# Branch A's gate product moved into the SSD stage, branch B's merge gate into pairs of seven products beside those of u

## The chip, the cores and the metric

The kernel runs on one core of one Trainium2 chip. The metric is the device time of one execution in microseconds (us); the time before is the median of three runs. The engines are named as in the profile: PE is TensorE's matmul, PEld its weight load, DVE VectorE, ACT ScalarE, POOL GpSimd, SP SyncE, which issues most of the loads.

## The reference, cut to what matters

One layer of three parallel branches for 576 tokens (512 of a prompt, 64 of a sample), with D = 1024. All columns that the branches need come from one product of the normed tokens with `w_in`:

```python
hn = _rmsnorm(x, norm_g)
proj = hn @ w_in
u, v, gate_a, z, xbc, dt_raw, q, gate_x, merge = jnp.split(proj, _split_points(IN_SIZES), axis=-1)
u = jax.nn.gelu(u, approximate=False)
v = _layernorm(jax.nn.gelu(v, approximate=False), ln_v_g, ln_v_b)
h_a = u * _gmlp_spatial(v, w_spatial, b_spatial) * jax.nn.silu(gate_a)       # branch A
...
h_b = _gated_group_rmsnorm(y.reshape(bsz, L, D_INNER).astype(x.dtype), z, ssd_norm_g)   # branch B
h_x = _mem_attention(q, mem_k, mem_v) * jax.nn.silu(gate_x)                  # branch X
g_a, g_b, g_x = jnp.split(jax.nn.sigmoid(merge), N_BRANCH, axis=-1)
m = g_a * (h_a @ w_proj_a) + g_b * (h_b @ w_proj_b) + g_x * (h_x @ w_proj_x)
return x + m @ w_out, ...
```

Two of these products matter here, each of 1024 columns: `gate_a` (branch A's gate, at column O_GA of `w_in`) and the second third of `merge` (the merge gate of branch B, at O_M + D).

## The kernel before

**Products.** Tokens and weights are each split into a high part and the rest, and a product of two tiles is made as high x high, high x rest and rest x high. The split of a weight tile is a cast on ACT (L98) and a subtraction on DVE (L99). A plain product of a tile of 128 columns with the 576 tokens is two halves of 288 tokens with 24 matmuls each (8 blocks of the inner size, three products of parts): 96 for two tiles. `wino` makes a pair of tiles, 256 columns, out of seven products of 12 matmuls each, 84 in all; for it DVE makes four sums of weight blocks (S, L904 to L907), all of these are split, sums of token blocks stand ready in `tT` (made once by `token_sums`, which also overwrites a quarter of `hn_hi` and `hn_lo`), and DVE and ACT put the seven results together (L935 to L947). `wino_th` is a `wino` followed by a tanh.

**Stage B** comes first, branch B's SSD in eight groups. Its PE order is written out by hand: the stage is a list of jobs (`conv_job` four to a group, for the next group; `z_job` two; `proj_job`; `gate_job`), each of two halves of 24 matmuls (line L167 in the rows). A job's weights are loaded two jobs ahead and split one job ahead. Between halves stand the small steps of the group's chunks, `w[0]` to `w[11]` of `steps`; the numbers in `PLACES` say after which half of the group each is put (without an entry: 0, 1, 2, 4, 5, 7 and so on). Groups 0 and 1 have 12 halves, the others 16. In the last group, which has no next group, four `gate_job`s stand where the others have convolutions, and four more follow in a tail, with the steps left of group 7 among them. Then the last round of `proj_job` (r = 3) makes the end of branch B's projection and stores it to a scratch in DRAM, `m_scr`, by way of ACT's queue (L766). Before, these `gate_job`s make the merge gate of branch B: their tanh stays in SBUF in buffers that are free by then (`gate_th`), and one DVE instruction per half in the last `proj_job`s (L764) applies it.

**Stage A** follows (from L870). The order here is the program's text, which a scheduler refines. It runs `v_block` (two, with `v_sample`), the memory's keys and values (`kv_block`, two, L1120), `v_norm` (L1141), the eight `spatial` steps (L1161) into `SP`, then four `ga_pair`, each two plain products of branch A's gate with its tanh and a DVE instruction per half (`gate2`), and a DVE instruction that multiplies `SP` by the gate (L1199), and then four `u_pair`: a `wino` of u, a gelu, the product with `SP` (L1204) and a split into `ha`. `token_sums` runs beside the first `ga_pair`. Then `m_sb` is loaded from `m_scr`, and pairs of branch A's merge gate and of its projection alternate.

After it come branch X, the merge and the output product; neither of them is touched.

**Line numbers.** The rows below and the first of each two pieces of order have the lines of the kernel before. In the changed kernel the helpers (L98, L99) and stage B stand two lines further down, `wino` one line. A plain product in stage A has the line L154, one of `wino`'s matmuls L925.

Of the kernel before, what the change touches and what calls it, by code (L numbers as in the profile page):

```python
# [42 lines left out]
def tile_hybrid_step(  # L43
# [144 lines left out]
    with ExitStack() as stb:  # L188
# [530 lines left out]
        def gate_job(jj):  # L719
            k = {}  # L720

            def load():
                if jj % 2 == 0:
                    gate_th["w", jj // 2] = load_block(w_in2, 0, KD, [(O_M + D + jj * P, 256)])

            def prep():
                k["w"] = wsplit(gate_th["w", jj // 2], KD, (jj % 2) * P)

            def half(f):
                if f == 0:  # L730
                    if jj < 3:
                        if jj == 0:
                            gate_th["x"] = pb.tile([P, 3, TW], F32, tag="xs", name="thx", bufs=2)
                        gate_th[jj] = gate_th["x"][:, jj, 0:T]
# [4 lines left out]
                S.activation(gate_th[jj][:, sl], ps, AF.Tanh, scale=0.5)
            return Job(load, prep, half)  # L740

        def proj_job(r, p):
# [10 lines left out]
            def half(j):  # L753
                jj = 2 * p + j
                w = [t[:, :, j * P:(j + 1) * P] for t in k["w"]]
                for f in range(2):
# [6 lines left out]
                    if r == 3:  # L763
                        V.scalar_tensor_tensor(dst, gate_th[jj][:, sl], 1.0, dst, ALU.add, ALU.mult)  # L764
# [112 lines left out]
    def token_sums(tile_):  # L877

        F = []
        for i, (k0, h) in enumerate(((0, 0), (0, 1), (4, 1), (4, 0))):  # L880
            sl = slice(h * HT, (h + 1) * HT)
            F.append(tile_().rearrange("p r t -> p (r t)").rearrange("p (k t) -> p k t", k=4))
            V.tensor_tensor(F[i], hn_hi[:, k0:k0 + 4, sl], hn_lo[:, k0:k0 + 4, sl], ALU.add)
        V.tensor_tensor(F[0], F[1], F[0], ALU.subtract)
        V.tensor_tensor(F[1], F[2], F[1], ALU.subtract)
        V.tensor_tensor(F[2], F[2], F[0], ALU.subtract)
        V.tensor_tensor(F[3], F[3], F[2], ALU.subtract)
        for i in range(3):
            split(F[i + 1], tT[:, i, 0], tT[:, i, 1])
        return F[0]  # L890
# [84 lines left out]
    with ExitStack() as sta:  # L975
# [177 lines left out]
        def tile_gemm(raw, j, xh, xl):  # L1153
            t = w_slot().rearrange("p r (k c) -> p r k c", k=KD)
            split(raw[:, :, j * P:(j + 1) * P], t[:, 0], t[:, 1])
            return gemm((t[:, 0], t[:, 1]), KD, xh, xl)

# [353 lines left out]
```

## Time and profile before

| | us |
|---|---|
| median of 3 runs (lowest, highest) | 1127.05 (1125.96, 1128.54) |
| the profiled execution: its own time | 1126.1 |
| the profiled execution: span from the first to the last instruction | 1124.4 |
| PE busy in the span | 1094.3 (97%) |
| DVE busy | 780.7 (69%) |
| ACT busy | 618.0 (55%) |
| mean granted TensorE clock | 0.998 |

The profiled execution's own time is 1.7 us more than its span, and 0.95 us under the median. Durations below come from this one execution. An idle time stands in brackets before the instruction that ended it, with what released that instruction.

### The profile page before, as it was taken

Reading aid. Unit: us, or ns where it says so; the run is one execution under the profiler, and the core shown is the slowest. Engines: PE = TensorE matmul, PEld = TensorE weight load, DVE = VectorE, ACT = ScalarE, POOL = GpSimd, SP = SyncE. Lnnn points to the kernel's source line nnn. Section 1 sums busy time; section 2 is a strip of 40 time slices with the busy share of each in tenths; the row PEclk is TensorE's granted clock in tenths of the full one; section 3 lists DMA queues with packets and bytes.
Section 4 is the critical chain, followed back from the end, with each engine's and each line's share of the span. In section 5 each row is a group of like instructions: output and inputs, shape, how many; then the busy total and the mean of one; then the engine's idle time right before and its main releaser. Section 6 shows DMA issues by size and latency. Waiting matters only on the chain.

```text
span 1124.4 us, 20432 instructions
## 1 busy us (share of the span) xinstructions
PE 1094.3 (97%) x8200; PEld 1017.2 (90%) x8200; DVE 780.7 (69%) x1444; ACT 618.0 (55%) x1291; POOL 25.0 (2%) x109
## 2 busy tenths in 40 slices
PE   5999999999999999999999999999999999999997
PEld 3999898999999998999999777999999998889776
DVE  5779797768687886876536536877965567765743
ACT  6466787768767576774542335425643336565421
POOL 1010000000000000000000000000000000000000
PEclk9999999999999999999999999999999999999999
DMA  5343535353544534354324325441352453556311
GB/s 175 114 102 113 152 107 150 115 146 83 166 130 128 131 100 137 99 164 131 99 95 158 133 75 178 150 150 39 112 198 97 155 162 113 151 160 215 133 47 75
DMA packets 160334, 144.38 MB, mean 128 GB/s; under 512 B 10152, under 2 KB 141264, under 8 KB 160240
## 3 DMA queue, kind: packets, MB, share of 16 engines
q1 hardware_dynamic: 137136, 125.60, 36.8%
q10 hardware_dynamic: 23104, 17.49, 4.9%
q8 instruction: 64, 1.05, 0.4%
q14 instruction: 30, 0.25, 0.1%
HBM read 123.61 MB, written 19.46 MB: 127 GB/s over the span
## 4 chain that ended last, share of the span: by engine, by line
PE 89%; DVE 4%; ACT 3%; DMA 2%; issue 1%; SPq 0%; ACTq 0%; DVEq 0%
PE acc L167 36%; PE acc L925 16%; PE acc L154 12%; PE acc L1055 4%; PE acc L1460 4%; PE acc L1120 2%; DMA e<-a_scr 2%; PE yps L555 1%; PE sps L651 1%; PE sps L510 1%; PE sps L574 1%; PE sps L599 1%; PE yps L1408 1%; PE yps L1161 1%; PE yps L1066 1%; PE sps L539 1%
## 5 line engine op out<-in xcount | busy, mean ns | idle before, releaser
L167 PE MATMUL acc<-hn_hi,whi 128*128 128x288 f32 x896 | 270.2, 302 | 0.2 <-DVE zs L471 0.2
L167 PE MATMUL acc<-hn_lo,whi 128*128 128x288 f32 x896 | 264.2, 295 | 0.0
L167 PE MATMUL acc<-hn_hi,wlo 128*128 128x288 f32 x896 | 264.0, 295 | 0.0
L167 PEld LDWEIGHTS acc<-hn_hi,whi 128*128 128x128 f32 x896 | 168.2, 188 | 2.3 <-issue 1.2
L167 PEld LDWEIGHTS acc<-hn_lo,whi 128*128 128x128 f32 x896 | 168.4, 188 | 0.4
L167 PEld LDWEIGHTS acc<-hn_hi,wlo 128*128 128x128 f32 x896 | 168.1, 188 | 0.1
L98 ACT CAST w<-wraw 128x1024 fp32r<-128x1024 f32 (+1 forms) x64 | 59.2, 942 | 103.3 <-PE acc L925 24.0
L99 DVE TENSOR_TENSOR wlo<-wraw,whi 128x1024 fp32r<-128x1024 f32 x72 | 87.9, 1221 | 30.3 <-ACT whi L98 29.8
L167 PE MATMUL acc<-hb,whi 128*128 128x288 f32 x512 | 104.6, 299 | 0.1
L98 ACT CAST whi<-wraw 128x1024 fp32r<-128x1024 f32 x72 | 75.6, 1050 | 41.3 <-PE acc L167 38.8
L99 DVE TENSOR_TENSOR w<-wraw,w 128x1024 fp32r<-128x1024 f32 x64 | 68.5, 1087 | 36.0 <-ACT w L98 35.8
L925 PE MATMUL acc<-hn_hi,w 128*128 128x288 f32 x512 | 89.5, 300 | 0.0
L925 PE MATMUL acc<-tT,w 128*128 128x288 f32 x576 | 86.1, 298 | 0.0
L426 DVE SCALAR_TENSOR_TENSOR cacc<-raw,cwh,cacc 128x600 f32<-128x600 f32 x96 | 80.5, 838 | 3.7 <-ACT cacc L424 2.8
L167 PEld LDWEIGHTS acc<-hb,whi 128*128 128x128 f32 x512 | 81.6, 188 | 1.0 <-issue 0.6
L925 PEld LDWEIGHTS acc<-tT,w 128*128 128x128 f32 x576 | 78.5, 188 | 0.9 <-issue 0.9
L925 PEld LDWEIGHTS acc<-hn_hi,w 128*128 128x128 f32 x512 | 74.0, 188 | 2.1 <-DVE thx L943 0.3
L167 PE MATMUL acc<-hb,wlo 128*128 128x288 f32 x256 | 75.3, 294 | 0.0
L99 DVE TENSOR_TENSOR w<-S,w 128x1024 fp32r<-128x1024 f32 x32 | 39.2, 1224 | 25.1 <-ACT w L98 25.1
L499 ACT ACTIVATE e<-e,nacs 128x128 f32<-128x128 f32 (+1 forms) x160 | 50.0, 382 | 8.6 <-DVE e L497 8.5
L154 PE MATMUL acc<-ha,w 128*128 128x288 f32 x384 | 51.6, 295 | 0.0
L154 PEld LDWEIGHTS acc<-ha,w 128*128 128x128 f32 x384 | 51.2, 189 | 0.0
(394 smaller groups left out, 2116.0 us busy)
## 6 DMA issues: line engine op xcount, KB each, us to landing
wraw<-in_w_in_dram SPq DMA_DIRECT2D x44, 1024.0 KB
wraw<-in_w_in_dram SPq DMA_DIRECT2D x16, 512.0 KB
e<-a_scr SPq DMA_DIRECT2D x32, 256.0 KB
h<-in_state_ssm_dram SPq DMA_DIRECT2D x16, 512.0 KB
out_dram<-h ACTq DMA_DIRECT2D x16, 512.0 KB
wraw<-in_w_proj_b_dram SPq DMA_DIRECT2D x8, 1024.0 KB
ebc<-e_scr SPq DMA_DIRECT2D x16, 288.0 KB
wraw<-in_w_mem_kv_dram SPq DMA_DIRECT2D x4, 1024.0 KB
```

The costliest lines, as they stand in the source:

```text
L98: S.copy(hi, v)
L99: (e or V).tensor_tensor(lo, v, hi, ALU.subtract)
L154: PE.matmul(ps[:n, :width], lhsT=a, rhs=b[:, sl], start=(i == 0), stop=(i == last))
L167: PE.matmul(ps[:, 0:HT], lhsT=a[:, k], rhs=b(k)[:, sl], start=(n == 0), stop=(n == 3 * nk - 1))
L426: V.scalar_tensor_tensor(a[:, 0:n], raw[:, i:i + n], cwh[:, i, q:q + 1], a[:, 0:n], ALU.mult, ALU.add)
L499: S.activation(e[:, h, 0:w], e[:, h, 0:w], AF.Exp, bias=nacs[:, c, h0_ + h:h0_ + h + 1])
L510: PE.transpose(tp[:, j * P:(j + 1) * P], xs[:, j, c0:c0 + P], ident)
L539: PE.matmul(cb[:, 0:w], lhsT=xs[:, 2, c0:c0 + P], rhs=CF[:, c0:c0 + w], start=True, stop=True)
L925: PE.matmul(ps[:, 0:HT], lhsT=w[:, r, k], rhs=x(q, k), start=first and n == 0, stop=n == 11, skip_group_check=True)
L1055: PE.matmul(pss[i], lhsT=x(k)[:, c], rhs=w[:, r, k2], start=(k + q == 0), stop=(k == KD - 1 and q == 2))
L1120: PE.matmul(pss[i], lhsT=x[xr], rhs=w[:, r, k2], start=(k + q == 0), stop=(k == KD - 1 and q == 2))
L1460: PE.matmul(ps[:, 0:cn], lhsT=x(k)[:, c], rhs=w, start=(k + q == 0), stop=(k == KD - 1 and q == 2))
```

## The change

**Branch A's gate** goes into stage B. `gate_job` now makes tiles of O_GA, plain; per half ACT makes the tanh, a DVE instruction the gate's value (the tanh plus one, times the product), and ACT's queue stores it to a new scratch `g_scr`, 16 stores in all. Tile 0 stands as the last job of group 0, tile 1 as the second of group 1, tiles 2 and 3 in group 7, and 4 to 7 in the tail. So groups 0 and 1 have 14 halves and group 7 has 12. In group 1 the last convolution job now closes the group, with z's second tile ahead of it. `PLACES` is new for group 1, group 2 takes the usual numbers, and in group 7 a step stands behind every half; `norm_y(7)` comes one half earlier in the tail.

**Branch B's merge gate** goes into stage A. `gate_b(p)` is a `wino_th` of O_M + D, a load of two tiles of `m_scr`, one DVE instruction that multiplies them, and a store to a new scratch `mb_scr`, from which `m_sb` is then loaded. It stands behind `u_pair(p)`, so that u and gate alternate. `u_pair` loads its part of `g_scr` and multiplies `SP` by it itself. The four `ga_pair` and the 16 DVE instructions of L764 are gone.

**Order in stage A.** `token_sums` runs behind the first v block, its splits behind the second; `v_norm` comes ahead of both `kv_block`s, and `spatial` ahead of the second one.

```diff
@@ stage B
+    g_scr = dpool.tile([P, KD, T], F32, name="g_scr")
+    mb_scr = dpool.tile([P, KD, T], F32, name="mb_scr")
...
         def gate_job(jj):
...
-                    gate_th["w", jj // 2] = load_block(w_in2, 0, KD, [(O_M + D + jj * P, 256)])
+                k["raw"] = load_block(w_in2, 0, KD, [(O_GA + jj * P, P)])
...
-                S.activation(gate_th[jj][:, sl], ps, AF.Tanh, scale=0.5)
+                th = pb.tile([P, HT], F32, tag="th", name="th", bufs=2)
+                S.activation(th, ps, AF.Tanh, scale=0.5)
+                V.scalar_tensor_tensor(th, th, 1.0, ps, ALU.add, ALU.mult)
+                S.dma_start(out=g_scr[:, jj, sl], in_=th)
...
-                    if r == 3:
-                        V.scalar_tensor_tensor(dst, gate_th[jj][:, sl], 1.0, dst, ALU.add, ALU.mult)
...
-                c = [conv_job(g + 1, ci) for ci in range(4)] if g + 1 < G else [gate_job(0), gate_job(1), gate_job(2), gate_job(3)]
+                c = [conv_job(g + 1, ci) for ci in range(4)] if g + 1 < G else [gate_job(2), gate_job(3)]
                 if g == 0:
-                    return [z[0], *c, z[1]]
+                    return [z[0], c[0], z[1], c[1], c[2], c[3], gate_job(0)]
                 if g == 1:
-                    return [c[0], c[1], z[0], c[2], c[3], z[1]]
+                    return [c[0], gate_job(1), c[1], z[0], c[2], z[1], c[3]]
...
+                if g == G - 1:
+                    return [c[0], a[0], c[1], a[1], b[0], b[1]]
...
-            PLACES = {0: (3, 4, 5, 6, 7, 8, 9, 10, 11, 12, 13, 14), 1: (1, 3, 4, 5, 6, 7, 8, 9, 10, 12, 13, 14),
-                      2: (1, 3, 4, 5, 6, 7, 8, 9, 10, 11, 12, 13)}
+            PLACES = {0: (3, 4, 5, 6, 7, 8, 9, 10, 11, 12, 13, 14), 1: (1, 2, 3, 4, 5, 6, 8, 9, 10, 11, 12, 13),
+                      G - 1: tuple(range(12))}
...
-            tail = {0: [lambda: y_smp(G - 1), lambda: gate_y(G - 1)], 5: [lambda: norm_y(G - 1)]}
+            tail = {0: [lambda: y_smp(G - 1), lambda: gate_y(G - 1)], 4: [lambda: norm_y(G - 1)]}
@@ stage A
         v_sample(0, 1)
+        F = token_sums()
...
         v_sample(1, 1)
+        token_splits(F, (1, 2, 3, 0))
+        v_norm()
         kv_block(0, k_scr, mk_out)
-        v_norm()
-        kv_block(1, v_scr, mv_out)
         SP = mpool.tile([P, KD, T], F32, tag="m", name="SP")
         for j in range(KD):
             spatial(j)
...
+        kv_block(1, v_scr, mv_out)
+
+        def u_pair(p):
             G_ = u_tile("g")
-            for j in range(2):
-                gate2(pS["pool"], tile_gemm(raw, j, xh, xl), G_[:, j])
+            SY.dma_start(out=G_, in_=g_scr[:, 2 * p:2 * p + 2])
+            U = wino(in_block(O_U + 256 * p), u_tile("u"))
             sp = flat(SP[:, 2 * p:2 * p + 2])
             V.scalar_tensor_tensor(sp, sp, 0.5, flat(G_), ALU.mult, ALU.mult)
...
+        def gate_b(p):
+
+            mp = u_tile("g")
+            SY.dma_start(out=mp, in_=m_scr[:, 2 * p:2 * p + 2])
+            thb = wino_th(in_block(O_M + D + 256 * p), u_tile("u"))
+            V.scalar_tensor_tensor(flat(mp), flat(thb), 1.0, flat(mp), ALU.add, ALU.mult)
+            S.dma_start(out=mb_scr[:, 2 * p:2 * p + 2], in_=mp)
+
         for p in range(4):
             u_pair(p)
+            gate_b(p)
...
-            SY.dma_start(out=m_sb[:, 2 * p:2 * p + 2], in_=m_scr[:, 2 * p:2 * p + 2])
+            SY.dma_start(out=m_sb[:, 2 * p:2 * p + 2], in_=mb_scr[:, 2 * p:2 * p + 2])
```

How the change moves instructions shows at three places. The first is ACT's row at `norm_y(0)`, in group 1 (BT: a chunk's copy; rs: the root of norm_y; e: a chunk's decay; raw: the copy of a convolution's half). Before:

```order
L518 COPY BT<-sps 128x128
L470 ACTIVATE th<-acc 128x288
L98 CAST whi<-wraw 128x1024
L708 ACT_TABLE_LOAD
L708 ACTIVATE rs<-acc 128x288 x2
L499 ACT_TABLE_LOAD
L499 ACTIVATE e<-e,nacs 128x128 x4
L709 ACTIVATE rs<-rs 128x576
L412 COPY raw<-acc 128x288
```

The same place after:

```order
L520 COPY BT<-sps 128x128
L414 COPY raw<-acc 128x288
L710 ACT_TABLE_LOAD
L710 ACTIVATE rs<-acc 128x288
L501 ACT_TABLE_LOAD
L501 ACTIVATE e<-e,nacs 128x128 x4
L710 ACT_TABLE_LOAD
L710 ACTIVATE rs<-acc 128x288
L501 ACT_TABLE_LOAD
L501 ACTIVATE e<-e,nacs 128x64
L711 ACTIVATE rs<-rs 128x576
```

The two halves of rs now stand apart, with the decays between them, and four table loads stand where two stood; the same happens at `norm_y(1)`, and the program has 25 of them instead of 21.

The second is ACT's row from the last projection round of stage B into stage A (whi: the last weights of branch B's projection; w: the first weights of the v block; m_scr: a store by ACT's queue). Before:

```order
L98 CAST whi<-wraw 128x1024
L766 DMA m_scr<-m_sb 128x576 x2
L98 CAST whi<-wraw 128x1024
L766 DMA m_scr<-m_sb 128x576 x5
L98 CAST w_7951<-wraw 128x1024
L98 CAST w_7978<-wraw 128x1024
```

The same place after:

```order
L100 CAST whi<-wraw 128x1024
L761 DMA m_scr<-m_sb 128x576 x2
L100 CAST whi<-wraw 128x1024
L761 DMA m_scr<-m_sb 128x576 x4
L100 CAST w_7987<-wraw 128x1024
L761 DMA m_scr<-m_sb 128x576
L100 CAST w_8014<-wraw 128x1024
```

The first cast of the v block's weights moved ahead of the last of the eight stores.

The third is DVE's row in a u pair (L1199: SP times branch A's gate; L1204: u times SP; L904 to L907: the sums S; L937, L943, L945: results of the seven products). Before, from the last `ga_pair` into the first `u_pair`:

```order
L1199 SCALAR_TENSOR_TENSOR SP<-SP,g 128x1152
L937 TENSOR_TENSOR u<-acc,p_9108 128x288
L99 TENSOR_TENSOR w_9219<-S,w_9219 128x1024
L99 TENSOR_TENSOR w_9225<-S,w_9225 128x1024
L943 TENSOR_TENSOR u<-acc,p_9110 128x288
L904 TENSOR_TENSOR S<-wraw 128x512
L945 TENSOR_TENSOR u<-acc,u_9109 128x288
L99 TENSOR_TENSOR w_9222<-wraw,w_9222 128x512
L905 TENSOR_TENSOR S<-wraw 128x512
L906 TENSOR_TENSOR S<-S,wraw 128x512
L907 TENSOR_TENSOR S<-wraw,S 128x512
L99 TENSOR_TENSOR w_9339<-wraw,w_9339 128x1024
```

After, from the end of the first `u_pair` into the first `gate_b`:

```order
L1198 TENSOR_TENSOR u<-u,SP 128x1152
L938 TENSOR_TENSOR u<-acc,p_8781 128x288
L905 TENSOR_TENSOR S<-wraw 128x512
L906 TENSOR_TENSOR S<-wraw 128x512
L101 TENSOR_TENSOR ha<-u,ha 128x1152
L907 TENSOR_TENSOR S<-S,wraw 128x512
L944 TENSOR_TENSOR u<-acc,p_8783 128x288
L908 TENSOR_TENSOR S<-wraw,S 128x512
L101 TENSOR_TENSOR w_8891<-S,w_8891 128x1024
L946 TENSOR_TENSOR u<-acc,u_8782 128x288
L101 TENSOR_TENSOR w_8894<-wraw,w_8894 128x512
L101 TENSOR_TENSOR w_8897<-S,w_8897 128x1024
```

The end of a u pair (its product with SP, its split) now stands between the results and the sums of a gate's pair, where another u pair followed before.

## Rows read from the trace of the kernel before

**Rows 1.** The page's busy time of each engine (its first part), and the chain of work that ended last, by engine (its fourth part).

```profile
PE 1094.3 (97%) x8200; PEld 1017.2 (90%) x8200; DVE 780.7 (69%) x1444; ACT 618.0 (55%) x1291; POOL 25.0 (2%) x109
PE 89%; DVE 4%; ACT 3%; DMA 2%; issue 1%; SPq 0%; ACTq 0%; DVEq 0%
```

**Rows 2.** Busy time in stretches: the stretch, its length, then the busy time and the instructions of PE, PEld, DVE, ACT and POOL, the granted clock, the DMA share and GB/s. The first two are group 1 (from about 109 us) and most of group 2, the third most of group 7, the fourth the end of the v blocks and `kv_block`, the last one u pair.

```profile
100.00:150.00 50.00, 46.55 (x382) 42.91 (x381) 41.28 (x83) 37.11 (x92) 2.03 (x11) 1.00 0.45 125
150.00:200.00 50.00, 49.17 (x406) 46.28 (x407) 40.89 (x82) 38.12 (x96) 2.14 (x11) 1.00 0.48 144
500.00:550.00 50.00, 50.00 (x398) 48.94 (x395) 35.59 (x70) 26.55 (x60) 0.00 (x0) 1.00 0.37 106
650.00:700.00 50.00, 50.00 (x253) 38.77 (x252) 26.25 (x58) 22.89 (x31) 0.00 (x0) 1.00 0.44 143
...
781.35:792.62 11.27, 11.27 (x86) 11.15 (x85) 10.25 (x14) 7.09 (x11) 0.00 (x0) 1.00 0.30 95
```

**Rows 3.** The chain of work that ended last, in order of time: start, duration, what it was. One half of 24 matmuls in stage B; the end of stage B; PE in `kv_block`; the four `ga_pair`; the four `u_pair` with what follows them; one pair of the merge gate alone.

```profile
150.59 3.16 PE acc L167 x24
...
621.30 1.67 issue
...
714.98 51.08 PE acc L154 x384
766.06 65.78 PE acc L925 x492
...
870.46 11.27 PE acc L925 x84
```

**Rows 4.** The timeline of PE in groups 1 and 2 (117 to 207 us): every instruction group ahead of which PE was idle, with that time in brackets.

```profile
119.66 0.55 PE L510 MATMUL sps<-ident,xs 128*128 128x128 f32 x3 [0.78 <-DVE e L540]
128.90 0.66 PE L612 MATMUL sps<-ident,yos 128*128 128x128 f32 x4 [0.35 <-DVE e L540]
137.14 0.68 PE L599 MATMUL sps<-C,hT 128*128 128x128 f32 x4 [0.23 <-DVE hT L581]
140.12 0.40 PE L707 MATMUL acc<-qq,onesn 128*128 128x288 f32 x1 [0.94 <-DVE qq L99]
150.07 0.52 PE L510 MATMUL sps<-ident,xs 128*128 128x128 f32 x3 [1.20 <-DVE e L540]
...
177.08 0.55 PE L510 MATMUL sps<-ident,xs 128*128 128x128 f32 x3 [0.56 <-ACT h0T L653]
...
196.35 0.40 PE L167 MATMUL acc<-hn_hi,whi 128*128 128x288 f32 x1 [0.20 <-DVE zs L471]
204.63 0.68 PE L599 MATMUL sps<-C,hT 128*128 128x128 f32 x4 [0.67 <-DVE hT L581]
205.54 0.52 PE L510 MATMUL sps<-ident,xs 128*128 128x128 f32 x3 [0.23 <-issue]
```

**Rows 5.** The timelines of ACT and DVE at the last convolution job of groups 1 and 2: the copy of its second half out of PSUM, and the last write of its result C.

```profile
157.75 0.35 ACT L416 COPY raw<-acc 128x224 f32<-128x224 f32 x1 [0.28 <-PE acc L167]
167.90 0.22 DVE L434 SCALAR_TENSOR_TENSOR C<-raw,cacc 128x64 f32<-128x64 f32 x1
...
231.45 0.35 ACT L416 COPY raw<-acc 128x224 f32<-128x224 f32 x1 [0.61 <-PE acc L167]
237.75 0.23 DVE L434 SCALAR_TENSOR_TENSOR C<-raw,cacc 128x64 f32<-128x64 f32 x1
```

**Rows 6.** The timeline of ACT in group 1: a wait for a store of the convolution's state by its own queue, and the two table loads at `norm_y(0)`.

```profile
134.64 0.70 ACT L428 ACTIVATE raw<-cacc 128x600 f32<-128x600 f32 x1 [5.36 <-DMA out_dram<-co]
...
139.91 1.28 ACT L708 ACT_TABLE_LOAD   x1
141.20 0.71 ACT L708 ACTIVATE rs<-acc 128x288 f32<-128x288 f32 x2
141.93 1.28 ACT L499 ACT_TABLE_LOAD   x1
143.23 1.28 ACT L499 ACTIVATE e<-e,nacs 128x128 f32<-128x128 f32 x4
```

**Rows 7.** The timeline of ACT at the end of stage B (ACTq: what its queue issues, here the stores of `m_scr`).

```profile
609.56 13.10 ACTq L766 DMA_DIRECT2D m_scr<-m_sb  x5
622.70 3.90 ACT L98 CAST w<-wraw 128x1024 fp32r<-128x1024 f32 x4 [13.15 <-DMA m_scr<-m_sb]
```

**Rows 8.** The timeline of PE (first row) and of ACT around `kv_block` and `v_norm` in stage A.

```profile
680.81 14.32 PE L1120 MATMUL acc<-w,meT 128*128 128x512 f32 x60
...
687.69 3.50 ACT L1141 ACTIVATE vT<-vT,nm,nwt 128x1024 f32<-128x1024 f32 x3
...
693.31 1.25 ACT L1141 ACTIVATE vT<-vT,nm,nwt 64x1024 f32<-64x1024 f32 x1
```

**Rows 9.** The timeline of DVE in the `ga_pair`s and `u_pair`s: the product of SP with the gate and the instruction behind it, the product of u with SP, the split into ha, and the one idle time in a pair.

```profile
769.53 1.35 DVE L1199 SCALAR_TENSOR_TENSOR SP<-SP,g 128x1152 f32<-128x1152 f32 x1
770.80 0.45 DVE L937 TENSOR_TENSOR u<-acc,p 128x288 f32<-128x288 f32 x1
...
779.98 1.35 DVE L1204 TENSOR_TENSOR u<-u,SP 128x1152 f32<-128x1152 f32 x1
...
782.78 1.35 DVE L99 TENSOR_TENSOR ha<-u,ha 128x1152 fp32r<-128x1152 f32 x1
785.12 1.23 DVE L99 TENSOR_TENSOR w<-S,w 128x1024 fp32r<-128x1024 f32 x1 [0.98 <-ACT w L98]
```

More of the change, by code (lines that the diff above doesn't have):

```diff
@@ L875, in tile_hybrid_step, with token_sums, token_splits @@
     tT = pT.tile([P, 3, 2, 4, HT], F32R, name="tT")
-    def token_sums(tile_):
-        F = []
+    def token_sums():
+        F = mpool.tile([P, 4, 4 * HT], F32, tag="m", name="F")
         for i, (k0, h) in enumerate(((0, 0), (0, 1), (4, 1), (4, 0))):
[L881 to L890, printed above, removed]
+            V.tensor_tensor(F[:, i].rearrange("p (k t) -> p k t", k=4), hn_hi[:, k0:k0 + 4, h * HT:(h + 1) * HT],
+                            hn_lo[:, k0:k0 + 4, h * HT:(h + 1) * HT], ALU.add)
+        for a, b in ((0, 1), (1, 2), (2, 2), (3, 3)):
+            V.tensor_tensor(F[:, a], F[:, b], F[:, (0, 1, 0, 2)[a]], ALU.subtract)
+        return F
+    def token_splits(F, ts):
+        for i in ts:
+            f = F[:, i].rearrange("p (k t) -> p k t", k=4)
+            if i == 0:
+                split(f, hn_hi[:, 0:4, HT:T], hn_lo[:, 0:4, HT:T])
+            else:
+                split(f, tT[:, i - 1, 0], tT[:, i - 1, 1])
     A_, B_ = slice(0, HT), slice(HT, T)
@@ L1151, in tile_gemm @@
             return gemm((t[:, 0], t[:, 1]), KD, xh, xl)
[L1153 to L1156, printed above, removed]
         def spatial(j):
@@ L1190, in u_tile @@
             return pu.tile([P, 2, T], F32, tag=tag, name=tag, bufs=2)
-        def ga_pair(p):
-            raw = in_block(O_GA + 256 * p)
+        kv_block(1, v_scr, mv_out)
+        def u_pair(p):
             G_ = u_tile("g")
-            for j in range(2):
-                gate2(pS["pool"], tile_gemm(raw, j, xh, xl), G_[:, j])
+            SY.dma_start(out=G_, in_=g_scr[:, 2 * p:2 * p + 2])
+            U = wino(in_block(O_U + 256 * p), u_tile("u"))
             sp = flat(SP[:, 2 * p:2 * p + 2])
             V.scalar_tensor_tensor(sp, sp, 0.5, flat(G_), ALU.mult, ALU.mult)
-        def u_pair(p):
-            U = wino(in_block(O_U + 256 * p), u_tile("u"))
             S.activation(flat(U), flat(U), AF.Gelu)
-            V.tensor_tensor(flat(U), flat(U), flat(SP[:, 2 * p:2 * p + 2]), ALU.mult)
+            V.tensor_tensor(flat(U), flat(U), sp, ALU.mult)
             hi, lo = ha_tile("ha"), ha_tile("ha")
@@ L1207, in u_pair @@
             ha.append((hi, lo))
-        ga_pair(0)
-        t1 = token_sums(lambda: ha_tile("F", F32))
-        for p in range(1, 4):
-            ga_pair(p)
-        split(t1, hn_hi[:, 0:4, B_], hn_lo[:, 0:4, B_])
+        def gate_b(p):
[4 more added lines that the diff above has]
+            S.dma_start(out=mb_scr[:, 2 * p:2 * p + 2], in_=mp)
         for p in range(4):
             u_pair(p)
+            gate_b(p)
         m_sb = mpool.tile([P, KD, T], F32, tag="m", name="m_sb")
         for p in range(4):
-            SY.dma_start(out=m_sb[:, 2 * p:2 * p + 2], in_=m_scr[:, 2 * p:2 * p + 2])
+            SY.dma_start(out=m_sb[:, 2 * p:2 * p + 2], in_=mb_scr[:, 2 * p:2 * p + 2])
         def proj_a(p, th):
```

11 lines of the change are left out of this document (1 added, 10 removed).

## The prediction

> **What bounds the kernel now.** I read the page's busy times first, then the chain of work that ended last, then the stretches, and only then the idle times. PE is busy for 1094.3 of 1124.4 us, and it holds 89% of the chain [rows 1]. So the kernel is a queue of matmuls with some 30 us of gaps: an edit gains if it takes matmuls out or closes a gap in PE's row, and it loses if it opens one. Work that moves on DVE or ACT counts only where PE ends up waiting for it. The stretches tell where that threatens. In group 1 and the first part of group 2, PE is idle for 3.45 and 0.83 us in 50, with ACT busy for 37 to 38 and DVE for 41. In group 7 PE has no idle time, and DVE and ACT have room; so have they in the v blocks and `kv_block` (650 to 700). In a u pair PE is full, and DVE is busy for 10.25 of 11.27 us [rows 2].
>
> **Products.** The four `ga_pair` are 384 matmuls in 51.08 us [rows 3], 0.133 each. They go to stage B, where a half of 24 takes 3.16 us [rows 3], 0.132 each: 16 halves leave as the merge gate's and 16 come as branch A's gate. That count in stage B stands. The merge gate's own 384 matmuls become four pairs of 84, each 11.27 us [rows 3]: 45.1. So stage A loses 51.1 us and gets 45.1, and the sum begins with **-6.0**. The 48 matmuls are gone whatever the order, so this term is firm to some 0.2 us, as long as PE isn't made to wait.
>
> **The end of stage B.** ACT's queue issues the last five stores of `m_scr`, and the casts of the v block's first weights stand behind them; the first starts at 622.70, after 13.15 us of waiting [rows 7], and the chain has 1.67 us there in which PE waits for nothing shown [rows 3]. Now one cast stands ahead of the last store, and 16 DVE instructions fewer stand before the stores. PE's gap of 1.67 us and some of the ramp behind it should go: **-1.8**. It can't be more than 2.5 (the gap and as much as one store's issue), and not less than 0.5, because the last cast that PE needs at first is now free.
>
> **kv, v_norm, spatial.** PE ran 60 matmuls of `kv_block` in 14.32 us while ACT made `vT` [rows 8]. ACT finished the last `vT` at 693.31 + 1.25 = 694.56, and PE went on at 695.0. Now only the first block's 48 matmuls cover it: 48 x 14.32/60 = 11.5 us, up to 692.3. `v_norm` is begun a little earlier, ahead of the copies of the first block, which take 0.6 us each. I take a wait of **+0.8**, from 0 to 2.3 (694.6 - 692.3). `token_sums` and its splits, eight sums and four splits on 128 x 1152, 12 x 1.35 [rows 9] = 16 us of DVE, move from the gate pairs to the v blocks and `kv_block`. DVE is busy there for 26.25 of 50 us [rows 2], so I cost them at nothing; without that room one of them ahead of a split of weights would hold it for 1.35 us.
>
> **u and gate in turn.** This is the place where the change could undo itself. A u pair costs DVE 10.25 us with its overlaps [rows 2]. It now gets the product of SP with the gate, 769.53 to 770.80, so 1.27 from start to start [rows 9]: 11.52, more than the pair's 11.27 on PE. A gate's pair is the same without the product L1204 and the split, 2 x 1.27 less, but with one multiplication of 128 x 1152, 1.27 more: 8.98. Together 20.50 of 22.54 us: 91%. 2.04 us are to spare in each two pairs. What DVE also loses in a pair is its wait for ACT's cast of S, 0.98 [rows 9]; with two of these 0.08 is left. DVE is thus nearly the bound, but not quite, and both kinds of pair use ACT for about 7 of 11.27 us [rows 2]. The first u pair's product with SP also waits for a load from `g_scr` that can be issued only behind the last spatial step. I take **+0.8** for the four rounds, from 0 (DVE keeps up) to 4 (1 us in each).
>
> **Groups 1 and 2.** Three things act against each other. (a) Group 1 gets two more halves of 3.16 us between its steps. Its idle times are 0.78 + 0.35 + 0.23 + 0.94 + 1.20 = 3.5 us, those of group 2 0.56 + 0.20 + 0.67 + 0.23 = 1.7 [rows 4], and nearly all of them end on DVE's e, hT or qq, which more cover helps. I take -3.5, from -5.2 to 0. (b) The last convolution of group 1 now closes the group. From the copy of its second half to C there were 10.4 us (157.75 to 168.12) and in group 2 6.5 (231.45 to 237.98) [rows 5]. The first step of group 2 needs C after one more half, so after 3.2 us and some 1.5 of small steps. The wait is 10.4 - 4.7 = 5.7 or 6.5 - 4.7 = 1.8; since the copy now has fewer z steps beside it I take the smaller one, rounded up: +2. (c) ACT gets four more table loads of 1.28 us, 5.1, because the two halves of rs stand apart, and its queue stores of `g_scr`, next to which the row shows a wait of 5.36 us for a store [rows 6]. Behind each load stand decays (e) that PE needs a half later at the earliest, so most of it should be covered; I take +0.5, from 0 to 5.1. Together **-1.0**, from -5 to +5.
>
> In the rows, an activation starts 0.01 us after the table load before it ends (141.93 + 1.28 = 143.21, e at 143.23) [rows 6]. The Trainium skill ("ScalarE: Activation LUTs", section "What ACT_TABLE_LOAD costs") gives a load about 1.28 us and a drain of about 1.38 on top, 2.66 for a switch; by that the four switches would take 10.6 us of ACT, not 5.1, and this speaks against the change. The load agrees with the rows; a drain of that length isn't seen behind it, and a part of it could only lie ahead. By that page (c) could take 10.6 us where the sum has 0.5, if all of it reached PE: 1130.8; I give that 0.02, inside the slower cases.
>
> **Group 7.** The steps that had 16 halves between them now have 12, with one behind every half. Some chains get two halves of cover where they had three. PE has no gap there [rows 2], so there's nothing to gain; DVE's 35.6 of 50 us would rise by about a third. I take **+1.5**, from 0 to 4 (four steps that each wait about one us, as the two longest of [rows 4]). The tail's DVE instructions, 0.45 per half [rows 9], lie beside 3.16 us of PE.
>
> **Sum.** -6.0 - 1.8 + 0.8 + 0.8 - 1.0 + 1.5 = -5.7. The profiled execution took 1126.1 us, so 1120.4; it lies 0.95 under the median of the runs, so against that 1121.3. I give **1120.7**, between the two.
>
> **The rivals.** *DVE becomes the bound between u and gate* (slower). In the rows a u pair has one wait of DVE for ACT's cast. If the alternation brings it to four or five in each two pairs of 22.54 us (ACT has the gelu and the tanh as well, and the casts come later), DVE needs 20.50 + 4.5 x 0.98 = 24.9, and PE waits 2.4 us a round, 9.5 in all, where the sum has 0.8: 1120.7 + 8.7 = 1129.4, just slower. That is the point from which it decides; at six waits it's 1135. For it: 20.5 is the highest share of DVE that any stretch here has. Against: the merge gate's own pairs and the u pairs both run without a gap on PE now. Chance 0.08.
>
> *The gaps move to group 1, 2 and 7* (no change). Nothing of (a) is gained, (b) is 5.7 and (c) 2: +7.7 where the sum has -1.0, with the products and the rest as forecast: 1129.4 at the worst, 1125 with half of it. For it: ACT and DVE are busiest just here. Chance 0.17.
>
> *The gaps close* (faster by more). Groups 1 and 2 lose all of their 5.2 us, C comes in time, group 7 and the alternation cost nothing: -6.0 - 2.5 - 5.2 = -13.7 against 1126.6 (between the run and the median), 1113. With half of it, 1116.5. For it: most of the costs I added rest on covers that I counted in halves, and not on a wait in a row. Chance 0.20.
>
> That the change doesn't do what it says is excluded for the products, since the count is fixed.
>
> **How the numbers follow.** My forecast, 1118 to 1124, gets 0.53. 0.2% is 2.25 us, about what a measurement of this kernel can tell from no change: faster is under 1124.8, slower over 1129.3. The forecast and the faster rival are below 1124.8, 0.73, and a little of the second rival, so faster has 0.74. Same has 0.16, most of the second rival, and slower 0.10 (the DVE rival and the late tables). The range leaves out the ends of the rivals: 1114.5 to 1127.5.
>
> **What would show it.** Right: stage A's stretch from `spatial` to branch A's merge gate is 6 us shorter, with PE without idle time in it, and the cast into the v block has no wait of 13 us for a store. Wrong: idle time of PE in front of L925's matmuls with DVE as what ended it; a wait for C at the first step of group 2 of over 5 us; waits in group 7 of over 1 us each. What would upset the whole is a wait on the loads of `g_scr` or `m_scr` in the alternation, because SP's queue holds the weights behind them.

## The result and the profile after

The changed kernel takes 1134.08 us (median of four runs, 1133.51 to 1135.14) where the kernel before, measured beside it, took 1126.68: a ratio of 1.0067, 95% interval 1.0054 to 1.0080. It is slower by 7.4 us, where 5 to 6 us less had been forecast. The profiled execution took 1133.98 us, its span is 1132.2.

The first view is the page's busy time, against [rows 1]; then busy time in stretches, against [rows 2]: the stretch, its length, busy time and instructions of PE, PEld, DVE, ACT, POOL, the granted clock, DMA share, GB/s.

```profile
PE 1096.0 (97%) x8152; PEld 1019.9 (90%) x8152; DVE 797.1 (70%) x1468; ACT 635.7 (56%) x1307; POOL 24.8 (2%) x109
```

```profile
100.00:150.00 50.00, 46.70 (x373) 43.68 (x372) 38.61 (x78) 35.91 (x88) 3.19 (x11) 0.94 0.59 168
150.00:200.00 50.00, 43.74 (x345) 41.59 (x345) 33.99 (x66) 35.32 (x88) 1.22 (x8) 0.94 0.34 101
200.00:250.00 50.00, 45.99 (x330) 43.99 (x330) 35.05 (x70) 31.66 (x67) 0.97 (x6) 0.91 0.28 83
500.00:550.00 50.00, 50.00 (x420) 47.82 (x419) 39.43 (x80) 32.58 (x81) 0.79 (x4) 1.00 0.51 145
...
762.78:774.05 11.27, 11.27 (x87) 11.27 (x86) 11.27 (x15) 7.11 (x11) 0.00 (x0) 1.00 0.42 128
```

PE has 48 matmuls fewer and yet is busy for 1.7 us more. The reader should look at the counts: in 150 to 200 us PE did 406 instructions before and does 345 now. And the clock column, 1.00 in each row of [rows 2], is 0.91 to 0.94 in the first three here.

To find where the time went I compare marks that both kernels have: the first small step of groups 0, 3 and 7 (the product of C and x), the first matmul of `kv_block`, the first of branch A's projection. PE's timeline gives the first three, before and after:

```profile
74.25 0.38 PE L539 MATMUL sps<-C,xs 128*128 128x128 f32 x2
242.45 0.38 PE L539 MATMUL sps<-C,xs 128*128 128x128 f32 x2
506.91 0.38 PE L539 MATMUL sps<-C,xs 128*128 128x128 f32 x2
```

```profile
75.57 0.38 PE L541 MATMUL sps<-C,xs 128*128 128x128 f32 x2
272.67 0.38 PE L541 MATMUL sps<-C,xs 128*128 128x128 f32 x2
534.85 0.38 PE L541 MATMUL sps<-C,xs 128*128 128x128 f32 x2
```

and the chain gives the two others. Its first line here is of the kernel before, whose other mark is 766.06 + 65.78 = 831.84 [rows 3]; the three lines behind it are of the changed kernel. Of the 828 matmuls, 672 are the eight pairs of u and gate, and 156 follow them, as before the change:

```profile
680.88 14.25 PE acc L1120 x60
```

```profile
694.71 11.43 PE acc L1121 x48
...
728.97 110.52 PE acc L926 x828
839.49 0.13 PE acc L156
```

| stage | before, us | after, us | more | of it matmuls moved or saved | the rest | forecast of the rest |
|---|---|---|---|---|---|---|
| up to group 0's first step | 74.25 | 75.57 | +1.3 | 0 | +1.3 | 0 |
| groups 0 to 2 | 168.20 | 197.10 | +28.9 | +12.7 (4 halves) | **+16.2** | -1.0 |
| groups 3 to 6 | 264.46 | 262.18 | -2.3 | 0 | -2.3 | 0 |
| group 7 to the first of `kv_block` | 173.97 | 159.86 | -14.1 | -12.7 | -1.4 | -0.3 |
| to branch A's projection | 150.96 | 144.78 | -6.2 | -6.0 | -0.2 | +1.6 |
| the rest | 292.56 | 292.71 | +0.2 | 0 | +0.2 | 0 |

The loss lies in groups 0 to 2. (The 1.3 us ahead of them is no loss of the change: that stretch takes 73.9 to 76.7 us in the profiled executions of the runs below.) What was forecast for stage A, and for the way into it, came out within 2 us. PE's idle times there, against [rows 4], are fewer and longer:

```profile
144.65 0.61 PE L708 MATMUL acc<-qq,onesn 128*128 128x288 f32 x1 [2.98 <-ACT qq L100]
...
160.17 0.52 PE L512 MATMUL sps<-ident,xs 128*128 128x128 f32 x3 [3.88 <-issue]
...
197.83 0.46 PE L541 MATMUL sps<-C,xs 128*128 128x128 f32 x2 [2.38 <-DVE C L436]
...
231.89 0.40 PE L169 MATMUL acc<-hn_hi,whi 128*128 128x288 f32 x1 [2.47 <-ACT whi L100]
...
233.53 0.61 PE L169 MATMUL acc<-hn_hi,wlo 128*128 128x288 f32 x1 [1.11 <-DVE wlo L101]
```

From 76 to 290 us all idle times sum to 13.4 us (before 5.2): +8.2. The other half of the loss is the clock. Behind each of the four waits the matmuls take longer for a while: PE's timeline has 0.44 us for one, 0.24 from start to start, and then 0.29 and 0.132 again.

```profile
146.81 0.44 PE L169 MATMUL acc<-hn_hi,wlo 128*128 128x288 f32 x1
...
151.01 0.29 PE L169 MATMUL acc<-hn_hi,wlo 128*128 128x288 f32 x1
```

```profile
140.00:150.00 10.00, 6.83 (x42) 6.15 (x42) 4.48 (x9) 5.93 (x11) 0.00 (x0) 0.70 0.44 104
...
230.00:240.00 10.00, 6.99 (x30) 6.57 (x30) 7.67 (x15) 6.44 (x15) 0.00 (x0) 0.66 0.00 1
```

That is the lower of the clock's two levels, 1.2 instead of 2.4 GHz. Of the matmuls of the halves, 67 ran so (18, 14, 13 and 22 behind the four waits), before none: 67 x (0.240 - 0.132) = 7.2 us. With the idle time that's 15.4 of the 16.2.

What made ACT late in group 1 is in its own timeline, against [rows 6] (the last two rows are stretches around the loads, in the changed kernel and in the kernel before; ACT is the fourth engine):

```profile
143.57 0.31 ACTq L454 DMA_DIRECT2D out_dram<-co  x1
143.93 0.67 ACT L100 CAST qq<-zs 128x576 fp32r<-128x576 f32 x1 [4.37 <-DVE t L604]
...
145.27 1.28 ACT L710 ACT_TABLE_LOAD   x1
146.56 0.41 ACT L710 ACTIVATE rs<-acc 128x288 f32<-128x288 f32 x1
146.98 1.28 ACT L501 ACT_TABLE_LOAD   x1
148.27 1.28 ACT L501 ACTIVATE e<-e,nacs 128x128 f32<-128x128 f32 x4
149.57 1.28 ACT L710 ACT_TABLE_LOAD   x1
150.86 0.41 ACT L710 ACTIVATE rs<-acc 128x288 f32<-128x288 f32 x1
151.29 1.28 ACT L501 ACT_TABLE_LOAD   x1
...
146.00:157.00 11.00, 10.29 (x62) 9.99 (x60) 5.47 (x12) 10.91 (x21) 0.00 (x0) 0.78 0.02 4
```

```profile
140.00:151.00 11.00, 9.66 (x70) 9.16 (x71) 10.10 (x20) 9.30 (x19) 0.00 (x0) 1.00 0.42 126
```

Two things could do it: qq stands behind stores that ACT's queue issues (the row names a DVE instruction that ended long before; 0.05 us ahead of qq is a store), and four table loads stand in 8 us where two did. The third candidate is the convolution that closes group 1.

### The profile page after: what moved, and what is told of

The parts are those of the page before. It is cut to its first block, busy times and chain, and to the rows that moved or that the text cites. A ratio compares the mean times of both kernels' runs of the same rounds, so it can differ in the third digit from the quotient of the medians.

```text
span 1132.2 us, 20460 instructions
## 1 busy us (share of the span) xinstructions
PE 1096.0 (97%) x8152; PEld 1019.9 (90%) x8152; DVE 797.1 (70%) x1468; ACT 635.7 (56%) x1307; POOL 24.8 (2%) x109
## 5 line engine op out<-in xcount | busy, mean ns | idle before, releaser
L169 PE MATMUL acc<-hn_hi,wlo 128*128 128x288 f32 x896 | 267.8, 299 | 1.1 <-DVE wlo L101 1.1
L169 PEld LDWEIGHTS acc<-hn_hi,whi 128*128 128x128 f32 x896 | 171.6, 192 | 4.4 <-ACT whi L100 2.7
L926 PE MATMUL acc<-hn_hi,w 128*128 128x288 f32 x640 | 110.0, 299 | 0.0
L100 ACT CAST w<-wraw 128x1024 fp32r<-128x1024 f32 x64 | 58.1, 916 | 87.2 <-PE acc L926 28.4
L926 PE MATMUL acc<-tT,w 128*128 128x288 f32 x720 | 107.0, 298 | 0.0
L926 PEld LDWEIGHTS acc<-tT,w 128*128 128x128 f32 x720 | 98.1, 188 | 1.2 <-issue 0.9
L926 PEld LDWEIGHTS acc<-hn_hi,w 128*128 128x128 f32 x640 | 92.5, 188 | 1.8 <-DVE thx L944 0.3
L101 DVE TENSOR_TENSOR w<-S,w 128x1024 fp32r<-128x1024 f32 x40 | 48.9, 1222 | 26.6 <-ACT w L100 26.6
L100 ACT CAST w<-S 128x1024 fp32r<-128x1024 f32 x40 | 42.1, 1053 | 27.5 <-PE acc L156 18.4
L926 PE MATMUL acc<-hn_lo,w 128*128 128x288 f32 x320 | 56.1, 295 | 0.0
```

The source lines that it names most:

```text
L100: S.copy(hi, v)
L101: (e or V).tensor_tensor(lo, v, hi, ALU.subtract)
L169: PE.matmul(ps[:, 0:HT], lhsT=a[:, k], rhs=b(k)[:, sl], start=(n == 0), stop=(n == 3 * nk - 1))
L926: PE.matmul(ps[:, 0:HT], lhsT=w[:, r, k], rhs=x(q, k), start=first and n == 0, stop=n == 11, skip_group_check=True)
```

## The experiments

Each run is compared with the kernel before, measured beside it, which had medians of 1127.6 to 1128.3. A difference between two runs "by the ratios" is uncertain by some 2 to 3 us, since both ratios have an interval. "Loads" are ACT's table loads in the program, 25 in the changed kernel, 21 before.

**1. All gate tiles late.** The lists and `PLACES` of groups 0 to 2 and 7 as before the change, gates 0 to 3 in group 7, `norm_y(7)` at its old place in the tail; 21 loads.

```diff
-c = ... else [gate_job(2), gate_job(3)]
+c = ... else [gate_job(0), gate_job(1), gate_job(2), gate_job(3)]
-return [z[0], c[0], z[1], c[1], c[2], c[3], gate_job(0)]
+return [z[0], *c, z[1]]
-return [c[0], gate_job(1), c[1], z[0], c[2], z[1], c[3]]
+return [c[0], c[1], z[0], c[2], c[3], z[1]]
```

> Branch A's gate tiles 0 and 1 leave groups 0 and 1: all eight stand in the last group and the tail, with the order of groups 0 to 2 and 7 as before the change; stage A as after. Theory (the loss lies in groups 1 and 2: PE waits 13.4 us there instead of 5.2 and runs some 70 matmuls at half clock behind the waits): no stretch of 5 us under 0.9 of the clock there, 1118 to 1121 us. Rival (the loss comes with the alternation in stage A or with the added traffic, wherever the gate stands): over 1128 us.

1122.31 us, ratio 0.9951 (0.9936 to 0.9965), 5.3 us under the kernel before, and the clock doesn't fall. It is 1 us over what was expected, but the rival is out: the alternation and the added traffic cost nothing like 7 us.

**2. The stores by POOL's queue.**

```diff
-S.dma_start(out=g_scr[:, jj, sl], in_=th)
+GP.dma_start(out=g_scr[:, jj, sl], in_=th)
-S.dma_start(out=conv_p[0, 0, :, c0:c0 + P], ...)
+GP.dma_start(out=conv_p[0, 0, :, c0:c0 + P], ...)
-S.dma_start(out=cso[:, c0:c0 + P], ...)
+GP.dma_start(out=cso[:, c0:c0 + P], ...)
```

> The changed kernel, but the stores of the convolution's state and of g_scr are issued by POOL's queue and not by ACT's. Theory that ACT is late because its queue waits for these stores: the waits at norm_y(0) (3.2 us) and at the weights' cast in group 2 (3.6 us) shrink to under 1 us, with their slow clock: 1123 to 1127 us. Rival (the table loads and the order of ACT's work make it late): within 2 us of the changed kernel, 1132 to 1135.

1124.51, ratio 0.9971 (0.9956 to 0.9985). The wait for qq is gone; the wait at 160 us is left with 1.9 us (here for BT), those for the weights with 1.9 and 1.1, and that for C with 2.4. But the new order of ACT has 23 loads, so this run moved two things and decides nothing alone.

**3. norm_y ahead of the decays**, so the two halves of rs stay together: 21 loads.

```diff
-w[3] = [chunk_cb(g, 2), y_off(g, 1), yd(g, 0, 1), decays(g, 3)]  +  [norm_y(g - 1)]
+w[3] = [chunk_cb(g, 2), y_off(g, 1), yd(g, 0, 1)]  +  [norm_y(g - 1)]  +  [decays(g, 3)]
```

> The changed kernel, with norm_y written ahead of the decays in its step, so that the two halves of rs stay together on ACT and the program has 21 table loads again, not 25. Theory that the four table loads (5.1 us of ACT) are what PE waits for at 160 and at 232 us: these two waits (3.9 and 3.6 us) go with their slow clock, 1122 to 1126 us. Rival (the stores of ACT's queue): the first wait stays and the time is over 1130.

1122.41, ratio 0.9952 (0.9935 to 0.9968): some 12.6 us less than the changed kernel (7.4 above the kernel before against 5.2 under it), from moving one step within a list. The waits at 160 and at 232 us are gone; of PE's waits in groups 1 and 2 two of over 1 us stay, as expected of the loads' theory. The third row is ACT's cast of qq, which ends the first of them, and here the profile names a store of the convolution's state (`out_dram<-co`) as what held it:

```profile
142.46 0.40 PE L708 MATMUL acc<-qq,onesn 128*128 128x288 f32 x1 [2.59 <-ACT qq L100]
...
189.38 0.46 PE L541 MATMUL sps<-C,xs 128*128 128x128 f32 x2 [2.37 <-DVE C L436]
...
141.73 0.67 ACT L100 CAST qq<-zs 128x576 fp32r<-128x576 f32 x1 [3.98 <-DMA out_dram<-co]
```

**4. The convolution ahead of z's second tile.**

```diff
-return [c[0], gate_job(1), c[1], z[0], c[2], z[1], c[3]]
+return [c[0], gate_job(1), c[1], z[0], c[2], c[3], z[1]]
```

> The changed kernel, with the last convolution of group 1 ahead of z's second tile again. Theory: only the wait for C at the first step of group 2 (2.4 us and about 1.5 of slow clock) goes: 1129 to 1131 us. Rival (what waits is only moved to the next step, since ACT is late anyway): 1133 to 1135.

1132.15, ratio 1.0038 (1.0025 to 1.0052): 3 us less than the changed kernel by the ratios. The wait for C is gone, but the wait at 160 us grew from 3.9 to 5.0 and the idle time is 13.4 us as before it; in the trace groups 0 to 2 are 1.7 us shorter, which is what the slow matmuls behind that wait had cost. A bit of both, then.

**5. Filler ahead of the waits**: matmuls into a bank of PSUM that nobody reads; they are extra work.

```diff
+def filler(n):
+    ps = acc_tile()
+    for _ in range(n):
+        PE.matmul(ps[:, 0:HT], lhsT=onesn, rhs=xh(0)[:, 0:HT], start=True, stop=True)
...
+if g == 1: w[3].insert(-1, lambda: filler(22)); w[5].insert(2, lambda: filler(40))
+if g == 2: w[0].insert(0, lambda: filler(18)); w[5].append(lambda: filler(20))
```

> The changed kernel with matmuls whose result nobody reads put ahead of four of PE's waits (22 and 40 in group 1, 18 and 20 in group 2), about as long as the waits were; they end no wait. Theory that the slow clock follows from PE standing idle: no stretch of 5 us in groups 1 and 2 falls under 0.9, and the time falls by part of the 7 us that matmuls at half clock cost, to 1127 to 1131 us, though PE does 100 matmuls more. Rival (the clock falls for another reason, or ACT alone sets the pace so that a faster PE only waits longer): 1133 to 1136.

1132.64, ratio 1.0041 (1.0028 to 1.0054), 2.9 us less than the changed kernel by the ratios, a bit over the range expected. In groups 1 and 2 no matmul of the halves runs at the lower level, and groups 0 to 2 take 192.7 us, 4.4 less, with 100 matmuls more:

```profile
100.00:150.00 50.00, 48.86 (x404) 45.81 (x403) 39.13 (x80) 35.14 (x86) 3.23 (x11) 1.00 0.59 168
150.00:200.00 50.00, 48.77 (x402) 46.57 (x400) 33.90 (x66) 36.20 (x91) 1.22 (x8) 1.00 0.36 102
200.00:250.00 50.00, 48.21 (x376) 46.49 (x375) 36.51 (x73) 34.71 (x73) 1.94 (x9) 1.00 0.36 100
```

So in this kernel the clock falls because PE stands idle. What that costs is 4.4 of the 7.2 us counted by the traces, 2.9 by the medians; that the rest would have been waiting for ACT is argued, not shown.

**6 and 7. Stores by POOL, one logarithm**, the second with the convolution moved as well.

```diff
-S.activation(rs[:, sl], ms[:, 0:HT], AF.Ln)      # in the loop over the halves
+V.tensor_copy(rs[:, sl], ms[:, 0:HT])
+S.activation(rs, rs, AF.Ln)                      # behind it
```

> The changed kernel with both mends: stores of the convolution's state and of g_scr by POOL's queue, and one logarithm over both halves of rs (two DVE copies out of PSUM ahead of it), so 21 table loads. If the two causes add, of the waits of groups 1 and 2 only that for C (2.4 us) stays: 1117 to 1120 us. If they hide each other: about 1122.

> The same with the last convolution of group 1 ahead of z's second tile. Theory: the wait for C goes too and all of PE's gaps in groups 1 and 2 are under 1 us each: 1114 to 1117 us. Rival (the order of the changed kernel suits the other steps better): no better than the run before it, 1118 or more.

1121.74, ratio 0.9941 (0.9925 to 0.9956), and 1118.19, 0.9915 (0.9893 to 0.9936). They are 1.7 and 1.2 us over their ranges; runs 10 to 12 show a reason.

**8. The kernel before, with the convolution's stores by POOL's queue.**

> The kernel before with the stores of the convolution's state by POOL's queue: the control for the two runs before. If ACT's queue costs the kernel before as well (5.4 us of waiting in group 1, of which PE has its gaps of 0.9 and 1.2): 1124 to 1126 us. If it only matters where ACT is late already: within 1 us of before.

1132.19, ratio 1.0033 (1.0020 to 1.0046): slower, which neither expected. Its longest new wait is one of 2.7 us in group 0 for a chunk's copy, with DVE and ACT behind loads of the decays, and 21 matmuls behind it run at the lower level; groups 0 to 2 are 5.3 us longer in the trace. Whether POOL's queue did it, or the order that the scheduler made of ACT's work, isn't settled.

**9. Run 3 with four loads more**: a logarithm of one column in the middle of a decay, which nothing uses, in groups 1 and 2; 25 loads.

```diff
+if g in (1, 2) and c == 3 and h == 1:
+    S.activation(lj, e[:, 0, 0:1], AF.Ln, scale=0.0, bias=1.0)
```

> The run with norm_y ahead of the decays (21 table loads, 1122.4 us), plus one logarithm of a single column in the middle of a decay in groups 1 and 2, which nothing uses: two table loads more in each, 25 in all, the order of the rest as it was. Theory that the loads themselves make ACT late: the waits of PE behind norm_y(0) and norm_y(1) return with their slow clock, 1129 to 1135 us. Rival (the order of the decays did it, the loads are covered): 1122 to 1125.

1131.91, ratio 1.0031 (1.0021 to 1.0042), 9 us over run 3 from four loads of 1.28 us. The waits are back, and 55 matmuls at the lower level with them:

```profile
157.19 0.52 PE L515 MATMUL sps<-ident,xs 128*128 128x128 f32 x3 [2.86 <-ACT BT L523]
...
227.30 0.52 PE L515 MATMUL sps<-ident,xs 128*128 128x128 f32 x3 [1.52 <-issue]
229.15 0.40 PE L169 MATMUL acc<-hn_hi,whi 128*128 128x288 f32 x1 [1.33 <-ACT whi L100]
```

**10 to 12. One logarithm alone**, then with the convolution moved, then in the kernel of run 1.

> The changed kernel with one logarithm over both halves of rs (two DVE copies ahead of it), decays and stores as in the changed kernel: 21 table loads. Theory of the loads: like the run with norm_y ahead of the decays, 1121 to 1124 us, with the waits for qq and for C left. Rival (the order of the decays): 1130 or more.

> The same with the last convolution of group 1 ahead of z's second tile; stores on ACT's queue. If the wait for C (2.4 us and some 1.5 of slow clock) is a cost of its own: 3 to 4 us under the run before it, 1117 to 1120. Beside the run with POOL's queue (1118.2) it tells what that queue is worth: under 1.5 us by the theory that stores matter little once the loads are gone, 3 us or more if they are a cause of their own.

> All eight gate tiles late (groups 0 to 2 and 7 ordered as before the change), with one logarithm over both halves of rs as well. It had 21 table loads already, so by the theory that only the count of loads matters it stays within 2 us of 1122.3. If the two DVE copies cost or the single activation saves something by itself, it moves by more. It also tells whether gate tiles in groups 0 and 1 are worth anything once mended: the run before it should then be 2 us or more faster.

1125.23, ratio 0.9978 (0.9967 to 0.9990); 1122.66, 0.9956 (0.9941 to 0.9971); 1132.06, 1.0048 (1.0030 to 1.0066). So run 10 is 10 us under the changed kernel by the ratios, with the decays and the stores where they were: a second sign, beside run 3, that the loads are the cause, though it is 1.2 us over its range. The last is 10 us over run 1 by the medians (5.6 by the two traces, which caught run 1's slowest execution and run 12's fastest), and its count of loads is the same. The edit between them, 16 DVE copies and one logarithm in place of two, does that: the copies take 0.45 us each, and ACT's logarithms wait for them, 9.2 us in all. In the first rows below (run 12 and run 1, 300 to 350 us) PE has lost 2 us of 50 in a stretch in which the two programs differ by this edit alone; in group 1 PE waits for DVE:

```profile
300.00:350.00 50.00, 47.94 (x375) 45.92 (x375) 39.73 (x77) 32.33 (x72) 1.35 (x8) 1.00 0.41 117
```

```profile
300.00:350.00 50.00, 50.00 (x402) 48.53 (x402) 43.31 (x88) 35.15 (x81) 1.22 (x8) 1.00 0.36 100
```

```profile
159.46 0.64 PE L541 MATMUL sps<-C,xs 128*128 128x64 f32 x2 [2.43 <-DVE hT L583]
```

So runs 6, 7, 10 and 11 carry this cost too, and one logarithm was a poor way to test the loads; run 3 and run 9 are the clean pair. For the stores these runs are a clean pair twice over: run 6 against 10, and run 7 against 11, differ by POOL's queue alone. That is worth 4.2 and 4.6 us by the ratios, and the wait for qq, 3.4 and 2.4 us in runs 10 and 11, is gone in 6 and 7. By run 11's own measure (3 us or more) the stores are a cause of their own.

**13 to 16. The mends without the copies**: run 3 with the convolution moved; run 3 with the stores of `g_scr` alone by POOL; everything (both kinds of stores by POOL, norm_y one place earlier still); run 13 with the stores of `g_scr` by POOL. All have 21 loads.

> norm_y ahead of the decays (21 table loads) and the last convolution of group 1 ahead of z's second tile; stores on ACT's queue, no copies. If the wait for C is a cost of its own: 3 to 4 us under the run with norm_y ahead alone (1122.4), so 1118 to 1120. Rival (as in the run that moved the convolution alone, the wait goes on to the next step): 1121 to 1123.

> norm_y ahead of the decays, and the stores of g_scr alone by POOL's queue, the convolution's state by ACT's as in the changed kernel. Theory that the added stores hold qq at norm_y(0): that wait (2.6 us) falls under 1 us and the time to 1118 to 1120. Rival (the eight stores of the convolution's state hold it, and stand there in any case): the wait stays over 2 us, 1121 to 1123.

> All mends without the DVE copies: norm_y ahead of the product that follows it and of the decays (21 table loads), both kinds of stores by POOL's queue, the convolution moved. The run with one logarithm had 1118.2 and lost about 1 us in each of the later groups to its copies: 1112 to 1116 us, no wait over 1 us in groups 1 and 2. Rival (POOL's queue costs what it cost the kernel before, 4 us): 1117 to 1120.

> norm_y ahead of the decays, the convolution moved, and only the stores of g_scr by POOL's queue. By the theory of the second run here 1115 to 1118, by its rival like the first run, 1118 to 1120.

| run | us | ratio to the kernel before | waits of PE over 1.2 us in groups 1 and 2 |
|---|---|---|---|
| 13 | 1119.80 | 0.9924 (0.9911 to 0.9937) | qq 3.1 |
| 14 | 1121.92 | 0.9951 (0.9938 to 0.9965) | qq 1.9, C 2.4 |
| 15 | 1115.69 | 0.9883 (0.9866 to 0.9899) | none |
| 16 | 1117.59 | 0.9905 (0.9892 to 0.9919) | qq 2.2 |

Run 13 is 3.2 us under run 3 by the ratios: with the loads gone, the wait for C is a cost of its own. It is also 3.0 us under run 1, so gate tiles in groups 0 and 1 are worth something once the loads and C are mended. Moving the stores of `g_scr` alone shortens the wait for qq from 2.6 to 1.9 us (run 3 to 14) and from 3.1 to 2.2 (run 13 to 16) and doesn't end it: the added stores hold the smaller part. (Run 16's time lies in the range of the theory that they hold it, but 2.1 us under run 13 is no more than the noise.) In runs 2, 6, 7 and 15, where the convolution's state is stored by POOL too, the wait is gone. Run 15's kernel is the fastest, 12.6 us under the one before, and its groups 1 and 2 look like this:

```profile
100.00:150.00 50.00, 49.26 (x408) 46.26 (x407) 43.06 (x88) 38.71 (x94) 9.15 (x23) 1.00 0.60 168
150.00:200.00 50.00, 49.60 (x409) 47.44 (x408) 39.96 (x80) 36.11 (x91) 1.71 (x11) 1.00 0.48 136
200.00:250.00 50.00, 50.00 (x420) 47.65 (x419) 37.37 (x72) 38.78 (x98) 7.05 (x16) 1.00 0.38 113
```

## Why the prediction was wrong

The step that failed is "Groups 1 and 2 ... Together -1.0, from -5 to +5", and in it above all the price of the table loads, (c). With group 0, which the steps' new places tie to it, it measured +16.2. Point by point:

- **Its (c), the table loads, +0.5 with an upper bound of 5.1.** This is the term that was missed. Removing the four loads by a change of order saved 12.6 us (run 3), and putting four back into that kernel cost 9 (run 9). I bounded their price by their own duration. But ACT was busy for 37 to 38 of 50 us [rows 2] and for 9.3 of 11 around the loads that stood there; with two more it is busy for 10.9 of 11, from 146 to 157 us. It had no room to catch up, and the lateness met PE further on, at 160 and 232 us: these are the waits that went in run 3 and came back in run 9. That it was handed on from step to step is read from this, not shown by itself. "Most of it should be covered" was reasoned from a half of cover for the first step behind the load, not for the steps behind that.
- **The clock** stood in no term. Four waits of 2.4 to 3.9 us were each followed by matmuls at half speed; 7.2 us by count, of which run 5 shows 4.4 to be a real cost. The kernel before had no wait over 1.2 us there [rows 4], so nothing in its rows of groups 1 and 2 showed it. By run 5's trace the 8.2 us more of waiting cost about 1.5 times their length.
- **Its (a), -3.5 from two more halves in group 1.** It didn't come, because ACT, not the number of halves, set the pace. Without the loads and with the stores and the convolution mended, the idle time from 76 to 290 us falls from 5.2 in the kernel before to 1.0 us (run 15), and groups 0 to 2 take 175.4 us, 5.5 less than before with the four halves counted: the -3.5 was there to be had.
- **Its (b), the wait for C, +2.** Measured 2.38, with 13 slow matmuls behind it; run 13 prices it at 3.2.
- **Its wait for stores.** PE's wait for qq, 3.0 us, is real, but runs 14 and 16 show that the stores there before hold it more than the added ones. What this costs here stood in no term; POOL's queue gives back 4 us (run 6 against 10, run 7 against 11).
- **The drain** that the Trainium skill adds to a table load ("ScalarE: Activation LUTs", section "What ACT_TABLE_LOAD costs"), to which I gave a chance of 0.02 at 1130.8. In the trace after, at `norm_y(0)`, a load begins 0.02 us after the instruction ahead of it ended (144.84 + 0.41 to 145.27) and the next begins 0.01 us after the load. So 1.28 us is the whole price on ACT here, and no drain is seen on either side. The rival's direction was right, its mechanism wasn't.

The rest held in its sum, in part by luck. **Products**: 828 matmuls in 110.52 us, 0.1335 each, and stage A's stretch is 6.2 us shorter. **kv, v_norm, spatial**: no wait of PE there, 0 where +0.8 was taken. **u and gate in turn**: DVE at 91% was forecast; it is busy for 93% of the eight pairs and in single pairs for all of 11.27 us, and PE waits for none of it, so +0.8 was 0. **The way into the v block** and **group 7** together gave -1.4 against -0.3, but the parts were off in opposite ways: the stretch behind the last matmul of stage B is 0.9 us shorter (forecast 1.8), and group 7 with the tail 0.5 shorter (forecast 1.5 longer). PE's gap of 1.67 us has shrunk to 0.63, and the wait of ACT's cast, 13.15 us [rows 7], is 9.44, still behind four stores of `m_scr`, so the prediction's sign (no wait of 13 us for a store) came true only in part:

```profile
633.76 1.05 ACT L100 CAST w<-wraw 128x1024 fp32r<-128x1024 f32 x1 [9.44 <-DVE m_sb L759]
...
638.43 0.73 PE L1056 MATMUL acc<-w,hn_hi 128*128 128x512 f32 x2 [0.63 <-DVE w L101]
```

None of the signs of being wrong came: no wait ahead of `wino`'s matmuls, none in group 7, and the wait for C was 2.4 us, not over 5. For the table loads, where the loss was, the prediction had set no sign. The rival that named DVE's bound as the slower case was wrong; the one that put the gaps into groups 1 and 2 had the place, but with 1129.4 at worst not the size, since it gave the table loads 2 us and the clock nothing.

## What to carry to other kernels

When an edit moves steps, print the order on every engine and look for pairs that were neighbours: two activations of one table set with another set's between them cost two loads more here, and on an engine that was three quarters busy their cost was not bounded by their own duration. Price a wait of the matmul engine at more than its length: in these runs most waits of 1.9 to 3.9 us were followed by matmuls at half speed. And when a change has several parts, run them apart before judging: here the part that was meant to gain did gain 5 to 6 us, and most of the loss came from an order that one line mends.

## What was not expected of the hardware

The clock didn't fall after each such wait. In the changed kernel and in runs 2 and 9 a wait of 2.4 us for C was followed by 12 or 13 slow matmuls, in runs 3, 10 and 14 the same wait (2.4 us) by none, while a wait of 1.9 us in run 14 was followed by 14; the runs don't say what decides. And a DVE copy of 128 x 288 twice in a group, 0.45 us each, slowed run 1's kernel by 10 us by the medians: more than the copies' own 7 us, on an engine that the changed kernel's page has at 70%.
